# A decoder layer on one core: GpSimd out of the two branch projections, operands split in whole quarters

## The chip, the cores and the metric

The kernel runs on 1 core of one Trainium2 chip. The metric is the device time in microseconds of one execution. A core has TensorE (PE, matrix products), VectorE (DVE), ScalarE (ACT), GpSimd (POOL) and SyncE (SP, which issues transfers), each with its own queue of instructions that it takes in order; they wait for each other through semaphores.

## The reference, cut to what matters

One layer of a decoder, 512 tokens by 1024 channels, all in float32:

```
h = x @ w_in                                 # nine groups of 1024 columns
ya = gelu(ua) * spatial(va) * silu(za)       # branch A
yb = rms_norm(diff_attention(q, k, v)) * silu(zb)   # branch B
merged = sigmoid(ga) * (ya @ w_branch_a) + sigmoid(gb) * (yb @ w_branch_b)
ple = sigmoid(x @ w_ple_gate) * (p @ w_ple)
out = layer_norm(alpha * x + merged @ w_out + ple)
```

## The kernel before, in words

**Products in three parts.** Each float32 operand is split into a high part (rounded to fp32r by ScalarE with a Copy activation) and a low part (what is left, a VectorE subtraction). A product of two operands is then three matrix products: high by high, high by low, low by high (`three`). The weights stream from HBM in units of 128 x 1024 (512 KB) into eight buffers `wr`, and are split into `wh` and `wl` (lines 409 and 412, `spread`), four buffers each. Where the text says product, it means one such TensorE instruction of 512 columns.

**Seven steps for eight.** Most projections of 512 x 1024 by 1024 x 1024 are done by `quad`: each operand is cut into quarters (11, 12, 21, 22), and seven block products of quarters and sums of quarters replace eight. A stage has seven steps of 24 products, 168 in all. The left operand needs four of its quarters' sums besides three quarters. For x, ya and yb they are

```
S1 = q21 - q22,  S2 = S1 - q11,  N4 = S2 + q12,  S3 = q11 - q21
```

and each is split into high and low as well. `xh` and `xl` hold x in quarters; once a quarter of x (and later of yb) is read for the last time, it is overwritten with a quarter of yb (and later of ya). The four sums stand in the tiles `xs` (`ys` is the same pair), slots 0 to 3. The sums of the weights' quarters are made in HBM ahead of time, or in the `wr` buffer itself by a transfer that adds the next quarter to it; GpSimd issues these accumulating transfers (`follow`, line 384) as soon as the low part of the old weights is made.

**The order of the work.** The tail of the kernel is a chain of stages: ga, gb (gates from x, whose sigmoids go to HBM), pg (the embedding's gate from x), ple (48 products with p), wb (yb by w_branch_b), wa (ya by w_branch_a), out (192 products of 512 columns and 48 of 256). All other work hangs on a clock that counts products: `later(n, f)` runs `f`, which appends its instructions to the engines' queues, after n more products have been issued. So a position, such as 84 in pg, says where an instruction stands in its engine's queue in relation to the products; an engine may still run ahead of or behind TensorE.

**The steps around the change.** `cut_part` splits half a quarter (128 x 512): ScalarE writes the high part, and four products later VectorE the low part (line 1211). `add` makes half a sum on GpSimd (line 1223), in place of a quarter of `ua` (which holds ya) or `yb`. In a stage, `block` (line 665) combines two results on VectorE and calls `done` two products later: a sigmoid on ScalarE for ga, gb and pg (lines 1197 and 1265); in wb a product with the gate (`mb_done`, line 1316, GpSimd for two blocks of eight); in wa `merge` (lines 1349 and 1350), a product with the gate and an addition of the wb result, with the additions for the first two token groups and two of the products on GpSimd. `MERGE` products after that, `merge_turn` transposes the block on TensorE (line 1356) into bank po or tr, from which ScalarE (line 1359) and VectorE (line 1360) write the parts of out's left operand. The gates come back from HBM through `load_gates` (line 1323, 512 KB for two token groups), ln_g and ln_b through `load_last` (line 1341), and x is added to `base` by four accumulating transfers of GpSimd (line 1293).

The positions of all this stand in constants, one or two numbers for each quarter:

```
YA22, YA_S1, YA_S3, YA_CUT_S1 = (170, 177), (180, 188), (196, 204), (200, 207)
YA11, YA12, YA_S2, YA_N4 = (26, 33), (50, 57), (44, 52), (68, 76)
```

The first line counts from pg's start (168 and more is in ple), the second from wb's start.

Of the kernel before, what the change touches and what calls it, by code (L numbers as in the profile page):

```python
# [25 lines left out]
NT = T // P  # L26
# [219 lines left out]
def hybrid_layer(ctx: ExitStack, tc: tile.TileContext, a, out: bass.AP):  # L246
    nc = tc.nc
    pe, dve, act, pool, sp = nc.tensor, nc.vector, nc.scalar, nc.gpsimd, nc.sync
# [238 lines left out]
    xh = big.tile([P, KT, T], F32R, name="xh", tag="X0")  # L487
    xl = big.tile([P, KT, T], F32R, name="xl", tag="X1")
# [137 lines left out]
    def pairs(turn):  # L626
        one, two = [pp(), pp()], [pp(), pbank("tx", 1)]
        return (one, two)[not turn], (one, two)[turn], [pbank("sc", 2) for _ in range(2)]

    def of_parts(h, l, k0, t0):  # L630
        def at(t, k):
            ts = slice(t0, t0 + 2 * P) if t is None else slice(t0 + t * P, t0 + (t + 1) * P)
            return h[:, k0 + k, ts], l[:, k0 + k, ts]

        return at

    def of_sum(parts, c):
        def at(t, k):
            ts = slice(0, 2 * P) if t is None else slice(t * P, (t + 1) * P)
            return parts[0][:, c, k, ts], parts[1][:, c, k, ts]  # L640

        return at

    def operands(h, l, parts, last=4):

        s1, s2, n4, s3 = parts if callable(parts[0]) else [of_sum(parts, c) for c in range(4)]
        return (of_parts(h, l, 0, 0), of_parts(h, l, 4, 0), s1, n4, s2, s3, of_parts(h, l, last, 2 * P))

    def quad(name, left, banks, place, done):
# [12 lines left out]
        def block(c, t, first, second, op, spare):  # L662
            z = place(c, t)
            z = spare if z is None else z
            dve.tensor_tensor(out=z, in0=first, in1=second, op=op)  # L665
            later(2, done, c, t, z, z)

        goes_on = name in GOES_ON

# [34 lines left out]
        for i, (bank, first, after) in enumerate(steps):  # L704
            w = next_pair(name, i)
            for t in range(2):
                if name == "zq":
                    for j, k in ((j, k) for j in range(2 - t) for k in range(4)):
                        h, l = w[k // 2]
# [3 lines left out]
                else:  # L713
                    for k in range(4):
                        h, l = w[k // 2]
# [246 lines left out]
    for k in range(KT):  # L962
        if k % 2 == 0:
            h, l = next_unit("kq")
# [14 lines left out]
    ua = big.tile([P, KT, T], F32, name="ua", tag="U")  # L979
# [10 lines left out]
    yb = []  # L990
# [28 lines left out]
    late = ctx.enter_context(tc.tile_pool(name="late", bufs=1, side="right"))  # L1019
# [182 lines left out]
    quad("ga", of_x, pairs(False), lambda c, t: None, gate_done("ga"))  # L1202
    ys = xs

    def part_of(tiles, k, t, part):
        return (tile[:, 4 * k + 2 * part:4 * k + 2 * part + 2, t * 2 * P:(t + 1) * 2 * P] for tile in tiles)

    def cut_part(source, where, part):
        h, l = part_of((xh, xl), *where, part) if where in ((0, 0), (1, 0), (0, 1), (1, 1)) else where(part)
        act.activation(h, source, AF.Copy)  # L1210
        later(CUT_LOW, lambda: dve.tensor_tensor(out=l, in0=source, in1=h.bitcast(F32), op=OP.subtract))

    def cut_yb(k, t, where, part):
        source, = part_of((yb[0],), k, t, part)
        cut_part(source, where, part)

    def cut_ya(k, t, where, part):
        source, = part_of((ua,), k, t, part)
        cut_part(source, where, part)

    def add(tile, to, op, x, y, part):
        (z,), (x,), (y,) = (part_of((tile,), *q, part) for q in (to, x, y))
        pool.tensor_tensor(out=z, in0=x, in1=y, op=op)

    def add_ya(*what):
        add(ua, *what)

    def add_yb(*what):
        add(yb[0], *what)

    def slot(c):
        return lambda part: (tile[:, c, 2 * part:2 * part + 2, :] for tile in ys)

    alone = []

    def first_sum(part):
        if not alone:
            alone.extend(late.tile([P, 4, 2 * P], F32R, name="ya" + n, tag=n) for n in "gb")
        return (tile[:, 2 * part:2 * part + 2, :] for tile in alone)

    def of_first_sum(t, k):
        return tuple(tile[:, k, t * P:(t + 1) * P] for tile in alone)

    def in_parts(fn, ats, *what):
        for part, n in enumerate(ats):
            later(n, fn, *what, part)

    in_parts(cut_yb, YB22, 1, 1, (0, 1))
    in_parts(add_yb, YB_S1, (1, 1), OP.subtract, (0, 1), (1, 1))
    in_parts(add_yb, YB_S3, (0, 1), OP.subtract, (0, 0), (0, 1))  # L1250
# [12 lines left out]

    def embedding_gate(c, t, z, source):
        act.activation(z, source, AF.Sigmoid)

    in_parts(cut_yb, YB11, 0, 0, (0, 0))
    in_parts(cut_yb, YB12, 1, 0, (1, 0))
    in_parts(add_yb, YB_S2, (0, 0), OP.subtract, (1, 1), (0, 0))
    in_parts(add_yb, YB_N4, (1, 0), OP.add, (0, 0), (1, 0))  # L1270
    in_parts(cut_yb, YB_CUT_S1, 1, 1, slot(0))
    in_parts(cut_yb, YB_CUT_N4, 1, 0, slot(2))
    in_parts(cut_yb, YB_CUT_S2, 0, 0, slot(1))
    in_parts(cut_yb, YB_CUT_S3, 0, 1, slot(3))
    in_parts(cut_ya, YA22, 1, 1, (1, 1))
    in_parts(add_ya, YA_S1, (1, 1), OP.subtract, (0, 1), (1, 1))
    in_parts(add_ya, YA_S3, (0, 1), OP.subtract, (0, 0), (0, 1))
    in_parts(cut_ya, YA_CUT_S1, 1, 1, first_sum)
    quad("pg", of_x, pairs(False), lambda c, t: base[:, t, c * T:(c + 1) * T], embedding_gate)


    gate = {}
# [14 lines left out]
    for c in (1, 0):  # L1297
        h, l = next_unit("ple")
# [8 lines left out]
    mb = []  # L1307
# [20 lines left out]
    in_parts(cut_ya, YA11, 0, 0, (0, 0))  # L1328
    in_parts(cut_ya, YA12, 1, 0, (1, 0))
    in_parts(add_ya, YA_S2, (0, 0), OP.subtract, (1, 1), (0, 0))  # L1330
    in_parts(add_ya, YA_N4, (1, 0), OP.add, (0, 0), (1, 0))
    in_parts(cut_ya, YA_CUT_S3, 0, 1, slot(0))
    in_parts(cut_ya, YA_CUT_N4, 1, 0, slot(2))
    in_parts(cut_ya, YA_CUT_S2, 0, 0, slot(1))
    quad("wb", operands(xh, xl, ys, 0), pairs(True), place_b, mb_done)

    norm_last = []
# [4 lines left out]

    later(LAST_NORM[0], load_last, "ln_g", "g")
    later(LAST_NORM[1], load_last, "ln_b", "b")

    def merge(c, t, z, source):
        early = t < NT // 2
        by = pool if early and c else dve
        by.tensor_tensor(out=z, in0=source, in1=gate.pop(("ga", c, t)), op=OP.mult)
        (pool if early else dve).tensor_tensor(out=z, in0=z, in1=mb[0][:, t, c * T:(c + 1) * T], op=OP.add)  # L1350
        later(MERGE["early" if early else c], merge_turn, c, t, z)

    def merge_turn(c, t, m):
        bank = pbank("tr" if t % 2 else "po", 1)
# [5 lines left out]
        later(3, lambda: dve.tensor_tensor(out=xl[:, at[0], at[1]], in0=turned,  # L1360
                                           in1=xh[:, at[0], at[1]].bitcast(F32), op=OP.subtract))
# [27 lines left out]
    for those in ((0, 1), (2, 3)):  # L1389
        banks = {t: pbank("sc", 2) for t in those} if those[0] else {0: pp(), 1: pbank("tx", 1)}  # L1390
        for k in range(KT):
# [9 lines left out]
            h, l = units[k // 2]  # L1401
# [10 lines left out]
    for t in range(NT):  # L1412
        ts = slice(t * P, (t + 1) * P)
        n = T if t < NT - 1 else T // 2
        for j in range(T // n):
            bank = pp()
            for k in range(KT):
# [4 lines left out]
                h, l = units[k // 2]  # L1422
# [46 lines left out]
```

## Time and profile before

| | |
|---|---|
| median of 3 runs | 621.21 us (620.9 to 624.6) |
| the profiled execution | 622.56 us, of which 620.8 us is the span of the trace |
| granted TensorE clock, mean | 0.996 |
| busy in the span | PE 607.7, DVE 470.4, ACT 338.3, POOL 156.6 us |
| stages by TensorE's starts | pg from 432.09, wb from 482.80, wa from 522.38 us; out's second group from 580.36 us |

Times in rows of the profile are microseconds from the start of the span. A row of the timeline has the start, the duration, the engine, the line, the operation and out<-in; in brackets stands how long the engine idled before it and what ended that. A row of the table by stretches has, for each engine, its busy time and its number of instructions, then the granted clock, the DMA engines' busy share and GB/s. Matrix products overlap each other, so a busy TensorE may still lose time, which is seen in the distance of two starts.

### The profile page before, as it was taken

The numbers are of one execution on the slowest core, as the hardware profiler recorded it, in microseconds if no ns is written. First come the engines' busy times: TensorE is split into PE (matmuls) and PEld (weight loads), VectorE is DVE, ScalarE is ACT, GpSimd is POOL, SyncE is SP. The second block draws the span as 40 slices with busy tenths as digits, with TensorE's granted clock in tenths as the row PEclk, the third lists the DMA queues.
The fourth block names the chain that finished last, engine by engine and source line by source line (L and its number), as shares of the span: only waits on it lengthen the run. The fifth ranks groups of instructions, "written<-read, shape, count | busy, mean of one in ns | idle before, by whom it ended". The sixth has DMA issues, their size and how long they took to land.

```text
span 620.8 us, 8616 instructions
## 1 busy us (share of the span) xinstructions
PE 607.7 (98%) x3012; PEld 508.5 (82%) x3012; DVE 470.4 (76%) x778; ACT 338.3 (54%) x542; POOL 156.6 (25%) x156
## 2 busy tenths in 40 slices
PE   9999999999999999999999999999999999998995
PEld 6888888888888888888899988888887787776884
DVE  6995687878888765748578987678799788658476
ACT  6656664645645654478665665546676554543200
POOL 1234011332432630230102121141423152443011
PEclk9999999999999999999999999999999999999998
DMA  8789889679797597668898898967976487999102
GB/s 288 237 242 190 259 288 268 246 188 290 267 255 273 177 295 223 160 183 300 272 311 191 244 226 241 234 173 232 232 205 195 178 235 208 255 224 267 33 34 102
DMA packets 45631, 138.52 MB, mean 223 GB/s; under 512 B 6036, under 2 KB 7188, under 8 KB 45268
## 3 DMA queue, kind: packets, MB, share of 16 engines
q1 hardware_dynamic: 35092, 102.71, 46.4%
q0 software_dynamic: 9920, 34.87, 30.7%
q8 instruction: 24, 0.39, 0.3%
q10 hardware_dynamic: 576, 0.39, 0.2%
q14 instruction: 19, 0.16, 0.1%
HBM read 118.95 MB, written 30.54 MB: 241 GB/s over the span
## 4 chain that ended last, share of the span: by engine, by line
PE 85%; DMA 6%; DVE 4%; issue 3%; ACT 1%; POOL 1%; DVEq 0%; SPq 0%; POOLq 0%; ACTq 0%
PE ps_pp L280 52%; PE ps_sc L280 15%; PE ps_tx L280 6%; PE ps_sc L801 3%; DMA wr<-in_w 3%; PE ps_po L846 3%; DMA gates<-gate_ga 1%; DVE wl L412 1%; PE ps_tr L835 1%; PE ps_po L280 1%; PE ps_tr L280 1%; DMA wr<-ws_wb 1%; DVE base L1290 1%; PE ps_tr L1172 1%; PE ps_po L1172 1%
## 5 line engine op out<-in xcount | busy, mean ns | idle before, releaser
L412 DVE TENSOR_TENSOR wl<-wr,wh 128x1024 fp32r<-128x1024 f32 (+1 forms) x143 | 190.2, 1334 | 45.6 <-ACT wh L409 43.4
L409 ACT ACTIVATE wh<-wr 128x1024 fp32r<-128x1024 f32 (+1 forms) x143 | 147.1, 1033 | 72.9 <-PE ps_sc L280 29.0
L280 PE MATMUL ps_pp<-xh,wh 128*128 128x512 f32 (+1 forms) x276 | 109.3, 397 | 0.0
L280 PE MATMUL ps_pp<-xl,wh 128*128 128x512 f32 (+1 forms) x276 | 107.0, 388 | 0.1
L280 PE MATMUL ps_pp<-xh,wl 128*128 128x512 f32 (+1 forms) x276 | 105.5, 383 | 0.0
L280 PE MATMUL ps_pp<-wh,xh 128*128 128x512 f32 (+1 forms) x168 | 64.0, 381 | 0.3 <-DVE s L665 0.2
L280 PE MATMUL ps_pp<-wh,xl 128*128 128x512 f32 (+1 forms) x168 | 64.2, 382 | 0.0
L280 PE MATMUL ps_pp<-wl,xh 128*128 128x512 f32 (+1 forms) x168 | 64.0, 381 | 0.0
L814 ACT ACTIVATE p<-p,sth 128x128 f32<-128x128 f32 (+3 forms) x64 | 35.5, 556 | 46.6 <-DVE sth L812 46.5
L384 POOL DMA_DIRECT2D wr<-in_w x34 | 29.6, 872 | 122.1 <-DVE wl L412 118.1
L280 PEld LDWEIGHTS ps_pp<-xh,wl 128*128 128x128 f32 x276 | 52.1, 189 | 8.9 <-DVE wl L307 0.2
L280 PEld LDWEIGHTS ps_pp<-xh,wh 128*128 128x128 f32 x276 | 52.0, 189 | 8.5 <-ACT wh L306 0.5
L280 PEld LDWEIGHTS ps_pp<-xl,wh 128*128 128x128 f32 x276 | 52.1, 189 | 8.3 <-DVE xl L307 0.4
L746 POOL TENSOR_TENSOR hl<-m,hl 128x512 fp32r<-128x512 f32 x16 | 25.1, 1627 | 54.4 <-ACT hl L741 54.4
L280 PEld LDWEIGHTS ps_pp<-wh,xh 128*128 128x128 f32 x168 | 31.6, 188 | 7.3 <-DVE s L665 0.6
L280 PEld LDWEIGHTS ps_pp<-wl,xh 128*128 128x128 f32 x168 | 31.6, 188 | 6.2 <-DVE wl L412 0.4
L280 PEld LDWEIGHTS ps_pp<-wh,xl 128*128 128x128 f32 x168 | 31.6, 188 | 5.7
L808 DVE CUSTOM_DVE_ANT_0 p<-ps_sc,mask 128x128 f32<-128x128 f32 (+3 forms) x64 | 30.9, 483 | 6.3 <-PE ps_sc L801 6.3
L280 PE MATMUL ps_sc<-wl,xsh 128*128 128x512 f32 x88 | 34.5, 392 | 0.6 <-DVE wl L412 0.6
L280 PE MATMUL ps_sc<-wh,xsh 128*128 128x512 f32 x88 | 34.3, 390 | 0.0
L280 PE MATMUL ps_sc<-wh,xsl 128*128 128x512 f32 x88 | 34.2, 389 | 0.0
L280 PE MATMUL ps_pp<-wh,xsh 128*128 128x512 f32 x80 | 31.4, 393 | 0.1
(315 smaller groups left out, 1268.1 us busy)
## 6 DMA issues: line engine op xcount, KB each, us to landing
wr<-in_w SPq DMA_DIRECT2D x81, 512.0 KB, 4.7
wr<-in_w POOLq DMA_DIRECT2D x30, 512.0 KB, 6.2
k<-hl SPq DMA_DIRECT2D x16, 256.0 KB, 5.4
q<-hl SPq DMA_DIRECT2D x16, 256.0 KB, 4.1
ws_va<-in_w POOLq DMA_DIRECT2D x8, 512.0 KB, 10.3
wr<-ws_va SPq DMA_DIRECT2D x8, 512.0 KB, 4.3
wa<-in_w POOLq DMA_DIRECT2D x6, 512.0 KB, 7.2
kx<-hl SPq DMA_DIRECT2D x12, 256.0 KB, 5.4
```

What stands on the lines that cost most here:

```text
L280: pe.matmul(ps, s, m, start=start, stop=stop, skip_group_check=read_within)
L384: pool.dma_start(out=raw[u][:, :n], in_=weights(STEPS[FOLLOWS[u]][1], n), accum_op=OP.add)
L409: act.activation(h, raw[u][:, :width(STEPS[u][0])], AF.Copy)
L412: dve.tensor_tensor(out=l, in0=raw[u][:, :width(STEPS[u][0])], in1=h.bitcast(F32), op=OP.subtract)
L746: pool.tensor_tensor(out=hl[:, 3 - j, :], in0=m[2 * j], in1=hl[:, j, :].bitcast(F32), op=OP.subtract)
L801: pe.matmul(sc[m][:, :n], q[:, m, i * P:(i + 1) * P], kk[:, m, :n], start=o == 0, stop=o == 1)
L808: dve.tensor_tensor_reduce(out=pr[m][:, :n], in0=sc[m][:, :n], in1=mask[:, T - n:], scale=-(DK ** -0.5), scalar=3e38, op0=OP.add, op1=OP.m ...
L814: act.activation(pr[m][:, :n], pr[m][:, :n], AF.Exp, bias=st[:, m:m + 1], scale=-1.0, accum_out=st[:, 2 + m:3 + m])
L835: pe.transpose(tr[:, j * P:(j + 1) * P], ad[:, j * P:(j + 1) * P], ident)
L846: pe.matmul(po[:, i * P:(i + 1) * P], at[:, j * P:(j + 1) * P], v[:, j, h * P:(h + 1) * P], start=j == 0, stop=j == i)
L1172: pe.matmul(sa[:, t * P:(t + 1) * P], va[:, t, g * P:(g + 1) * P], aux[0][:, 0, g, :], start=True, stop=True)
L1290: dve.scalar_tensor_tensor(out=z, in0=bank, scalar=1.0 / ALPHA, in1=z, op0=OP.mult, op1=OP.mult)
```

## The change

The two branch projections wb and wa no longer use GpSimd for arithmetic: the products with the gates and the additions in `mb_done` and `merge` are all VectorE's, and ya's sums S2 and N4, made in wb, are whole VectorE operations (an int in place of a pair of positions, `combine`). The sums of yb, and S1 and S3 of ya, stay on GpSimd in halves; the two of ya move from ple into pg. A quarter is split in one piece (128 x 1024) instead of two halves, for ya and yb alike.

Places and positions change too. The split ya22 goes to the tiles `yag` and `yab` in pg, and S1 takes its natural place in `xh` and `xl` in wb; before, S1 was in those tiles and ya22 in its natural place. So wa's third step reads S1 from `xh`/`xl` and its last reads ya22 from `yag`/`yab`. The split of yb's S3 moves from pg (150) to wb's product 10; those of ya's N4 and S2 move from wb into wa's products 4 and 28. The sigmoids of ga, gb and pg are queued 8 products after their block instead of 2. p is loaded at pg's product 34 for 64 and split at 60 and 72 for 104 and 116. ln_g and ln_b are loaded at out's products 4 and 16 for wa's 100 and 130. `MERGE` has a number for each block.

```
+SIGMOIDS = ('ga', 'gb', 'pg')
-YB22, YB_S1, YB_S3 = (60, 72), (80, 92), (104, 116)
-YB11, YB12, YB_S2, YB_N4 = (26, 33), (50, 57), (46, 58), (70, 82)
-YB_CUT_S1, YB_CUT_N4, YB_CUT_S2, YB_CUT_S3 = (75, 82), (101, 108), (124, 131), (150, 157)
-YA22, YA_S1, YA_S3, YA_CUT_S1 = (170, 177), (180, 188), (196, 204), (200, 207)
-YA11, YA12, YA_S2, YA_N4 = (26, 33), (50, 57), (44, 52), (68, 76)
-YA_CUT_S3, YA_CUT_N4, YA_CUT_S2 = (78, 85), (98, 105), (122, 129)
+YB22, YB_S1, YB_S3 = 60, (80, 92), (104, 116)
+YB11, YB12, YB_S2, YB_N4, YB_SUMS = 25, 49, (34, 46), (58, 70), (75, 101, 124, 226)
+YA22, YA_S1, YA_S3 = 36, (84, 96), (108, 120)
+YA11, YA12, YA_S2, YA_N4, YA_SUMS = 26, 50, 54, 64, (19, 76, 172, 196)
-LAST_NORM = (100, 130)
-MERGE = {'early': 24, 1: 23, 0: 22}
+LAST_NORM = (172, 184)
+MERGE = (36, 36, 25, 27), (40, 40, 68, 62)
...
-            later(2, done, c, t, z, z)
+            later(8 if name in SIGMOIDS else 2, done, c, t, z, z)
...
+    def quarter(tile, k, t):
+        return tile[:, 4 * k:4 * k + 4, t * 2 * P:(t + 1) * 2 * P]
+
+    def natural(k, t):
+        return lambda: (quarter(xh, k, t), quarter(xl, k, t))
...
+    def apart():
+        alone.extend(late.tile([P, 4, 2 * P], F32R, name="ya" + n, tag=n) for n in "gb")
+        return alone
...
+    def split_quarter(n, source, where):
+        def high():
+            h, l = where()
+            act.activation(h, source, AF.Copy)
+            later(CUT_LOW, lambda: dve.tensor_tensor(out=l, in0=source, in1=h.bitcast(F32), op=OP.subtract))
+
+        later(n, high)
+
+    def combine(ats, to, op, x, y):
+        def part(engine, e):
+            z, a0, a1 = (q[:, e] for q in (to, x, y))
+            engine.tensor_tensor(out=z, in0=a0, in1=a1, op=op)
+
+        if isinstance(ats, int):
+            later(ats, part, dve, slice(0, 4))
+        else:
+            for i, n in enumerate(ats):
+                later(n, part, pool, slice(2 * i, 2 * i + 2))
...
-            later(40 + 12 * k, cut, phl[0][:, 0, k, :], phl[0][:, 1, k, :], pt)
+            later(26 + 12 * k, cut, phl[0][:, 0, k, :], phl[0][:, 1, k, :], pt)
-    later(64, load_p)
+    later(34, load_p)
...
+    split_quarter(YB11, yb11, natural(0, 0))
+    combine(YB_S2, yb11, OP.subtract, yb22, yb11)
+    split_quarter(YB12, yb12, natural(1, 0))
+    combine(YB_N4, yb12, OP.add, yb11, yb12)
+    for n, source, c in zip(YB_SUMS, (yb22, yb12, yb11, yb21), (0, 2, 1, 3)):
+        split_quarter(n, source, slot(c))
+    split_quarter(YA22, ya22, apart)
+    combine(YA_S1, ya22, OP.subtract, ya21, ya22)
+    combine(YA_S3, ya21, OP.subtract, ya11, ya21)
     quad("pg", of_x, pairs(False), lambda c, t: base[:, t, c * T:(c + 1) * T], embedding_gate)
...
-        by = pool if c == 1 and t < 2 else dve
-        by.tensor_tensor(out=z, in0=source, in1=gate.pop(("gb", c, t)), op=OP.mult)
+        dve.tensor_tensor(out=z, in0=source, in1=gate.pop(("gb", c, t)), op=OP.mult)
...
+    split_quarter(YA_SUMS[0], ya22, natural(1, 1))
+    split_quarter(YA11, ya11, natural(0, 0))
+    combine(YA_S2, ya11, OP.subtract, ya22, ya11)
+    split_quarter(YA12, ya12, natural(1, 0))
+    combine(YA_N4, ya12, OP.add, ya11, ya12)
+    for n, source, c in zip(YA_SUMS[1:], (ya21, ya12, ya11), (0, 2, 1)):
+        split_quarter(n, source, slot(c))
     quad("wb", operands(xh, xl, ys, 0), pairs(True), place_b, mb_done)
...
-        early = t < NT // 2
-        by = pool if early and c else dve
-        by.tensor_tensor(out=z, in0=source, in1=gate.pop(("ga", c, t)), op=OP.mult)
-        (pool if early else dve).tensor_tensor(out=z, in0=z, in1=mb[0][:, t, c * T:(c + 1) * T], op=OP.add)
-        later(MERGE["early" if early else c], merge_turn, c, t, z)
+        dve.tensor_tensor(out=z, in0=source, in1=gate.pop(("ga", c, t)), op=OP.mult)
+        dve.tensor_tensor(out=z, in0=z, in1=mb[0][:, t, c * T:(c + 1) * T], op=OP.add)
+        later(MERGE[c][t], merge_turn, c, t, z)
...
-    of_ya = [of_first_sum, of_sum(ys, 1), of_sum(ys, 2), of_sum(ys, 0)]
-    quad("wa", operands(xh, xl, of_ya), pairs(False), lambda c, t: None, merge)
+    of_ya = (of_parts(xh, xl, 0, 0), of_parts(xh, xl, 4, 0), of_parts(xh, xl, 4, 2 * P),
+             of_sum(ys, 2), of_sum(ys, 1), of_sum(ys, 0), of_apart)
+    quad("wa", of_ya, pairs(False), lambda c, t: None, merge)
```

More of the change, by code (lines that the diff above doesn't have):

```diff
@@ L1203, in hybrid_layer @@
     ys = xs
[L1205 to L1229, printed above, removed]
+    def quarter(tile, k, t):
+        return tile[:, 4 * k:4 * k + 4, t * 2 * P:(t + 1) * 2 * P]
+    def natural(k, t):
+        return lambda: (quarter(xh, k, t), quarter(xl, k, t))
@@ L1231, in slot @@
     def slot(c):
-        return lambda part: (tile[:, c, 2 * part:2 * part + 2, :] for tile in ys)
+        return lambda: (ys[0][:, c], ys[1][:, c])
     alone = []
[L1236 to L1241, printed above, removed]
-        return tuple(tile[:, k, t * P:(t + 1) * P] for tile in alone)
-    def in_parts(fn, ats, *what):
-        for part, n in enumerate(ats):
-            later(n, fn, *what, part)
@@ L1248, in hybrid_layer, with of_apart @@
-    in_parts(cut_yb, YB22, 1, 1, (0, 1))
-    in_parts(add_yb, YB_S1, (1, 1), OP.subtract, (0, 1), (1, 1))
-    in_parts(add_yb, YB_S3, (0, 1), OP.subtract, (0, 0), (0, 1))
+    def apart():
+        alone.extend(late.tile([P, 4, 2 * P], F32R, name="ya" + n, tag=n) for n in "gb")
+        return alone
+    def of_apart(t, k):
+        return tuple(tile[:, k, t * P:(t + 1) * P] for tile in alone)
+    def split_quarter(n, source, where):
[4 more added lines that the diff above has]
+        later(n, high)
@@ new lines, in combine @@
+    def combine(ats, to, op, x, y):
[7 more added lines that the diff above has]
+                later(n, part, pool, slice(2 * i, 2 * i + 2))
+    yb11, yb12, yb21, yb22 = (quarter(yb[0], k, t) for t in range(2) for k in range(2))
+    ya11, ya12, ya21, ya22 = (quarter(ua, k, t) for t in range(2) for k in range(2))
@@ L1251, in hybrid_layer @@
+    split_quarter(YB22, yb22, natural(0, 1))
+    combine(YB_S1, yb22, OP.subtract, yb21, yb22)
+    combine(YB_S3, yb21, OP.subtract, yb11, yb21)
     quad("gb", of_x, pairs(True), lambda c, t: None, gate_done("gb"))
@@ L1265, in embedding_gate @@
         act.activation(z, source, AF.Sigmoid)
[L1267 to L1278, printed above, removed]
+    split_quarter(YB11, yb11, natural(0, 0))
[7 more added lines that the diff above has]
+    combine(YA_S3, ya21, OP.subtract, ya11, ya21)
     quad("pg", of_x, pairs(False), lambda c, t: base[:, t, c * T:(c + 1) * T], embedding_gate)
@@ L1327, in hybrid_layer @@
         later(n, load_gates, *what, i % 2)
[L1328 to L1334, printed above, removed]
+    split_quarter(YA_SUMS[0], ya22, natural(1, 1))
[5 more added lines that the diff above has]
+        split_quarter(n, source, slot(c))
     quad("wb", operands(xh, xl, ys, 0), pairs(True), place_b, mb_done)
```

## The prediction

> **What bounds the kernel now.** I read the head of the page first, then the chain that ended last, then TensorE's timeline by its starts.
>
> ```profile
> span 620.8 us, 8616 instructions
> ...
> PE 607.7 (98%) x3012; PEld 508.5 (82%) x3012; DVE 470.4 (76%) x778; ACT 338.3 (54%) x542; POOL 156.6 (25%) x156
> ```
>
> ```profile
> 444.04 10.88 PE ps_sc L280 x48
> ```
>
> TensorE is busy for 98% of the span, but one product's 0.39 us overlaps the next, so busy time hides gaps. The chain's piece gives the pace: 48 products in 10.88 us, 0.2267 us each. A stage of 168 products cannot take less than 38.08 us. The first products of wb, of wa and of out's second group stand here, and one transpose with the product behind it:
>
> ```profile
> 482.80 0.39 PE L280 MATMUL ps_pp<-wh,xh 128*128 128x512 f32 x1
> ...
> 522.38 0.39 PE L280 MATMUL ps_pp<-wh,xh 128*128 128x512 f32 x1
> ...
> 540.57 0.60 PE L1356 MATMUL ps_tr<-ident,s 128*128 128x128 f32 x4
> 540.92 0.48 PE L280 MATMUL ps_sc<-wl,xsh 128*128 128x512 f32 x1
> ...
> 580.36 0.39 PE L280 MATMUL ps_sc<-wh,xh 128*128 128x512 f32 x1
> ```
>
> wb takes 39.58 us, 1.5 over its floor. From 522.38 to 580.36 lie 168 + 48 products (48.97 us) and eight groups of transposes at 0.35 us (2.8 us): 57.98 us, 6.2 over. So 7.7 us is all that these stages can give. Four gaps (start to start, less 0.23) make most of it:
>
> ```profile
> 495.05 0.39 PE L280 MATMUL ps_sc<-wh,xsh 128*128 128x512 f32 x1
> 496.04 0.50 PE L280 MATMUL ps_sc<-wl,xsh 128*128 128x512 f32 x1 [0.60 <-DVE wl L412]
> ...
> 536.09 0.39 PE L280 MATMUL ps_sc<-wh,yag 128*128 128x512 f32 x1
> 537.29 0.66 PE L1356 MATMUL ps_po<-ident,s 128*128 128x128 f32 x4 [0.81 <-POOL s L1350]
> ...
> 559.12 0.39 PE L280 MATMUL ps_pp<-wl,xh 128*128 128x512 f32 x1
> 560.53 0.66 PE L1356 MATMUL ps_tr<-ident,s 128*128 128x128 f32 x4 [1.03 <-POOL s L1350]
> ...
> 569.04 0.39 PE L280 MATMUL ps_tx<-wl,xh 128*128 128x512 f32 x1
> 570.94 0.66 PE L1356 MATMUL ps_po<-ident,z 128*128 128x128 f32 x4 [1.51 <-DVE xl L1360]
> ```
>
> That is 0.76, 0.97, 1.18 and 1.67 us, 4.6 in all: a weight part late from VectorE, two transposes that wait for GpSimd's additions, and a transpose whose bank VectorE had not yet read.
>
> **GpSimd's price to VectorE.** Next I put POOL and DVE side by side:
>
> ```profile
> 412.26 4.25 POOL L1223 TENSOR_TENSOR yb<-yb 128x512 f32<-128x512 f32 x3
> 412.81 4.79 DVE L412 TENSOR_TENSOR wl<-wr,wh 128x1024 fp32r<-128x1024 f32 x1 [2.26 <-ACT wh L409]
> ```
>
> ```profile
> 479.76 1.29 POOL L1223 TENSOR_TENSOR ua<-ua 128x512 f32<-128x512 f32 x1
> ...
> 479.76 0.68 DVE L1290 SCALAR_TENSOR_TENSOR base<-ps_sc,base 128x512 f32<-128x512 f32 x1
> ```
>
> The weight part that takes 1.21 us elsewhere took 4.79: it ended 1.1 us after three GpSimd operations in a row. Line 1290, with one operand in PSUM, kept its 0.68 beside such an operation. So a GpSimd half quarter (1.29 us alone) holds up a VectorE operation with two SBUF operands by up to 1.3 us, more than the half would cost on VectorE.
>
> **The change, part by part.** Position n is n products into a stage.
>
> *wb and wa without GpSimd.* Two products with gates, four additions and two more products with gates move to VectorE at 0.69 us each, 5.5 us; four half sums become two whole ones, 2.4 us (1.21 each, the weight part's size). Twelve GpSimd operations go, each of which could hold VectorE for up to 1.3 us. VectorE's load is therefore about equal, and transposes now wait for an addition of 0.69 us, 36 to 68 products after its merge. The gaps 0.97 and 1.18 go; I take 0. The gap 0.76 comes from a VectorE that left ple full:
>
> ```profile
> core 0: us, PE busy (x) PEld busy (x) DVE busy (x) ACT busy (x) POOL busy (x), PEclk, DMA share, GB/s
> 433.30:443.30 10.00, 10.00 (x50) 8.43 (x49) 6.47 (x8) 5.91 (x9) 1.27 (x2) 1.00 1.01 262
> 443.30:453.30 10.00, 10.00 (x46) 8.29 (x45) 9.49 (x7) 7.31 (x11) 6.18 (x6) 1.00 0.83 205
> 453.30:462.30 9.00, 9.00 (x42) 7.44 (x41) 8.29 (x9) 6.14 (x9) 2.10 (x2) 1.00 0.94 227
> ...
> 471.60:482.70 11.10, 11.10 (x49) 8.99 (x49) 10.94 (x14) 5.37 (x8) 6.08 (x4) 1.00 0.51 169
> ```
>
> In ple VectorE was busy for 10.94 of 11.10 us; four half splits and four GpSimd halves leave it. But wb's first 64 products then carry six weight parts, four splits, two sums and two gate products: 12 x 1.14 + 2 x 0.6 = 14.9 us, and start near 2 us, for a part that is needed at product 79 (17.9 us). It just fits; 0 to 0.8, I take 0.3.
>
> *The last gap.* There VectorE stood at line 1349 for gates asked late, and the reading of the bank stood behind it:
>
> ```profile
> 544.79 0.86 POOL L384 DMA_DIRECT2D wr<-in_w  x1 [1.20 <-DVE wl L412]
> ...
> 560.42 3.55 POOL L1293 DMA_DIRECT2D base<-in_x  x4
> ```
>
> ```profile
> 559.80 0.39 SPq L1323 DMA_DIRECT2D gates<-gate_ga  x1
> ```
>
> ```profile
> 568.87 0.69 DVE L1349 TENSOR_TENSOR z<-ps_pp,gates 128x512 f32<-128x512 f32 x1 [1.60 <-DMA gates<-gate_ga]
> ```
>
> The load issued at 559.80 landed near 568.8, 9 us, beside four transfers of x issued at 560.42. GpSimd's queue will have nothing between 544.79 and these four, so they start some 15 us earlier, behind the last accumulation in their own queue, and SP's loads of ln_g and ln_b (LAST_NORM) go past the gates into out. The gates come sooner; the turns move from out's products 11 and 23 to 14 and 28, those of the other half column behind them to 35 and 41, so no bank is wanted again within 13 products. 0 to 1.7, I take 0.5. The remaining 7.7 - 4.6 = 3.1 us lie in small pieces, part of them bank waits that VectorE causes; I take 0.7 of them back.
>
> Gain: 4.6 - 0.3 - 0.5 + 0.7 = 4.5 us.
>
> *pg.* Into pg come ya22's split (36), all of S1 and S3 of ya on GpSimd (84 to 120), and the two cuts of p (60 and 72 for 104 and 116); out of it goes yb's S3. These lines are pg's VectorE before, and the start of its fifth step (the product's own line):
>
> ```profile
> 443.81 3.62 DVE L412 TENSOR_TENSOR wl<-wr,wh 128x1024 fp32r<-128x1024 f32 x1 [0.61 <-ACT wh L409]
> ...
> 447.35 0.68 DVE L1211 TENSOR_TENSOR xl<-yb,xh 128x512 fp32r<-128x512 f32 x1
> 447.95 1.21 DVE L412 TENSOR_TENSOR wl<-wr,wh 128x1024 fp32r<-128x1024 f32 x1
> 449.09 1.78 DVE L1211 TENSOR_TENSOR xl<-yb,xh 128x512 fp32r<-128x512 f32 x1
> ...
> 452.53 3.09 DVE L412 TENSOR_TENSOR wl<-wr,wh 128x1024 fp32r<-128x1024 f32 x1
> ...
> 458.49 1.21 DVE L412 TENSOR_TENSOR wl<-wr,wh 128x1024 fp32r<-128x1024 f32 x1
> ```
>
> ```profile
> 454.75 0.39 PE L280 MATMUL ps_pp<-wh,xsh 128*128 128x512 f32 x1
> ```
>
> Starts lie 0.60 us (half) and 1.14 us (whole) apart. The part at 458.49, ready at 459.7, is position 108's: the sixth step's second unit, needed 31 products after 454.75, at 461.8. Lead: 2.1 us. Ahead of it the new queue holds five whole splits for seven halves (5.7 for 4.2 us, 1.5 more), one more cut of p (0.6), and 7.5 GpSimd halves at 1.3 us (9.8; the first of S2 falls half beside a PSUM operation) where the old one lost 2.4, 1.1 and 1.9 us to four of them (the excess of 443.81, 449.09 and 452.53): 4.4 more. That is 6.5, less some 0.6 of idle time, 5.9. In program order S1's first half comes ahead of the accumulation at 84, and the other three follow it in a row, as the three at 412.26 did, just when positions 100 and 108 are due. TensorE then waits 5.9 - 2.1 = 3.8 us in pg. If the added halves fall into idle time, 1.5 us is left, inside the lead, and the cost is 0. Ends 0 and 3.8; I take 3.8, for the row at 412.26 has the same instructions in the same order. What VectorE owes is paid off by ple, which is relieved.
>
> *Costed at nothing.* Sigmoids at 8 for 2: ScalarE waited 10.3 us for VectorE in ga and gb, hidden under products; if that cover went, the price would be those waits. The loads of p go earlier in SP's queue, past nothing that TensorE needs soon. ln_g, asked at out's fourth product, waits there for wa's last step, whose operand lies in the tile that it overwrites; behind it stand ln_b and a weight load for out's second half, and if that were wanted at once, the price would be ln_g's wait.
>
> ```profile
> ACT s L1197 <- DVE s L665: 10.3, 9, 3.4
> ```
>
> Whole splits save starts (1.14 for 2 x 0.60), counted above. S1 of ya in its natural place and ya22 apart change no product; its last read merely lets the turns of the second column go earlier than the last step.
>
> **Sum.** -4.5 + 3.8 = -0.7 us. Against the profiled execution 622.56 - 0.7 = 621.9; that execution lies 1.35 over the median of the runs, so I forecast 621.21 - 0.7 = 620.5. I treat 1% (6.2 us) as what a measurement of this kernel can tell from no change.
>
> **Rivals.** *pg does not starve* (0.28): VectorE had 3.5 us idle from 433.3 to 443.3, and gb's stretched part stopped no product. Then 621.2 - 4.5 = 616.7; with all 7.7 us regained 613.5.
>
> *Slower: the early transfers of x* (0.11). Four times 512 KB at the 227 GB/s of the row from 453.30 are 9.2 us of traffic put into wa's sixth and seventh steps, beside out's weights and the last gates. If the queues share alike, half of it, 4.6 us, is added to the gates' 9: 13.6. Asked at 140 and held some 3 products by a weight part, they have 39 products and a group of transposes (9.2 us) less two VectorE operations (1.4) until the turn at 182. Beyond 7.8 us they decide; 5.8 us go to TensorE in place of the 0.5: 625.8. Against it: before, the four came 0.6 us after that load and shared with it already, and 1 MB of ln_g and ln_b leaves the stage.
>
> *Accumulations kept waiting* (0.03). More VectorE work on two SBUF operands in wa could hold up GpSimd's descriptors: one weight part's 1.14 us on each of three accumulated steps, with nothing to spare, makes 3.4 us, 623.9.
>
> ```profile
> L384 POOL DMA_DIRECT2D wr<-in_w x34: 837/861/1065, 50.2 to 544.8; - x34
> ```
>
> All 34 issues took 837 to 1065 ns, with VectorE busy or not. [...]
>
> **From these.** Forecast 0.58, the rivals 0.28, 0.11 and 0.03. The range is 615.8 to 624.6: below, pg's cost at 0 and 0.9 us more of the small pieces; above, wb's 0.8, the gates' 1.7 and none of the small pieces (622.9), and part of the way to the slower rivals. Faster by over 1% (under 615.0) needs nearly all 7.7 us and no cost in pg: 0.05. Slower by over 1% (over 627.4) needs pg's full cost, no gain and the early transfers: 0.03. Within: 0.92.
>
> **What would show it.** Right: weight parts of 4 us or more around pg's positions 84 to 110, TensorE gaps before "wl" there of 3 to 4 us, pg longer by 2 us or more, no wait for POOL at the transposes, wa within 1 us of its floor with transposes. Wrong: pg as long as before; a DVE wait for gate_ga over 2 us; a gap in wb's fourth step over 0.8 us. A lock that lets VectorE in between two GpSimd operations would make the pg term, and so the forecast, too slow.

## The result: 628.1 us, slower by 1%, and the profile after

The changed kernel takes 628.1 us in the median of four runs (627.35 to 629.4); the kernel before, on the same chip, 621.06 (620.75 to 624.6). The ratio is 1.0095, interval 1.0067 to 1.0124. I had forecast 620.5 and a range up to 624.6: wrong, and on the other side. The profiled execution took 627.35 us against 622.56, so 4.8 us have to be found in the trace. The head of the page after:

```profile
span 625.5 us, 8563 instructions
...
PE 608.3 (97%) x3012; PEld 511.2 (82%) x3012; DVE 470.0 (75%) x774; ACT 337.5 (54%) x528; POOL 136.7 (22%) x144
```

TensorE's busy time is as before, GpSimd's is down by 20 us, VectorE's is equal: the change did to the loads what it says. The time lies in TensorE's gaps. Its timeline after, at the two places that were lengthened, with the first product of out's second group at the end (columns: start and length in us, engine, line, operation, output and inputs; in brackets the idle time and what ended it):

```profile
462.15 0.39 PE L279 MATMUL ps_pp<-wh,xsh 128*128 128x512 f32 x1
464.00 0.50 PE L279 MATMUL ps_pp<-wl,xsh 128*128 128x512 f32 x1 [1.47 <-DVE wl L411]
...
465.04 0.39 PE L279 MATMUL ps_pp<-wh,xsl 128*128 128x512 f32 x1
466.70 0.50 PE L279 MATMUL ps_pp<-wh,xsh 128*128 128x512 f32 x1 [1.27 <-ACT s L659]
...
568.13 0.39 PE L279 MATMUL ps_pp<-wl,xh 128*128 128x512 f32 x1
573.07 1.09 PE L1345 MATMUL ps_po<-ident,z 128*128 128x128 f32 x4 [4.56 <-DVE z L1339]
...
574.38 0.63 PE L279 MATMUL ps_tx<-wh,xh 128*128 128x512 f32 x1
574.81 0.63 PE L279 MATMUL ps_tx<-wl,xh 128*128 128x512 f32 x1
...
585.03 0.39 PE L279 MATMUL ps_sc<-wh,xh 128*128 128x512 f32 x1
```

Start to start, less 0.23, the gaps are 1.62 and 1.43 us in pg and 4.71 us in out; behind the last one two products start 0.43 us apart where 0.23 is the pace. By stages, from the starts of their first products (for out, up to its second group):

| stage | before | after | difference | predicted |
|---|---|---|---|---|
| pg | 39.56 | 44.05 | +4.5 | +3.8 |
| ple | 11.15 | 11.15 | 0 | 0 |
| wb | 39.58 | 38.13 | -1.45 | -0.5 |
| wa | 43.93 | 40.03 | -3.90 | -2.8 with the 0.7 of small pieces |
| out, first group | 14.05 | 19.85 | +5.80 | -1.2 |

Ahead of pg the kernel after is 0.27 us sooner, and from the second group on both need 40.45 us. The other rows went the way that was forecast, pg near its size, wb and wa further than predicted. The one that turned the sign is the last row. VectorE's timeline after shows what stands at its head, and the queues of GpSimd and SP what came ahead of the load:

```profile
454.20 3.68 DVE L411 TENSOR_TENSOR wl<-wr,wh 128x1024 fp32r<-128x1024 f32 x2
457.80 5.01 DVE L1226 TENSOR_TENSOR xsl<-yb,xsh 128x1024 fp32r<-128x1024 f32 x1
462.74 1.21 DVE L411 TENSOR_TENSOR wl<-wr,wh 128x1024 fp32r<-128x1024 f32 x1
...
571.51 0.69 DVE L1338 TENSOR_TENSOR z<-ps_pp,gates 128x512 f32<-128x512 f32 x1 [6.12 <-DMA gates<-gate_ga]
```

```profile
454.06 1.60 POOL L1233 TENSOR_TENSOR ua<-ua 128x512 f32<-128x512 f32 x1
457.04 0.89 POOL L383 DMA_DIRECT2D wr<-in_w  x1 [1.39 <-DVE wl L411]
457.66 4.06 POOL L1233 TENSOR_TENSOR ua<-ua 128x512 f32<-128x512 f32 x3
...
546.48 3.94 POOL L1285 DMA_DIRECT2D base<-in_x  x4
```

```profile
559.58 0.43 SPq L1314 DMA_DIRECT2D gates<-gate_ga  x1
```

The four transfers of x go out at 546.48 instead of 560.42, right behind GpSimd's last accumulation. The gates of ga are asked at 559.58, as before (559.80), but VectorE can use them only at 571.51, after 11.9 us instead of 9. It stood 6.12 us for them; the transpose at 573.07 stood behind it. The transfers of x were still on their way when the gates were asked (their number, the shortest, median and longest issue in ns, the first and last start; then the shortest, median and longest time from issue to landing in us):

```profile
L1285 POOL DMA_DIRECT2D base<-in_x x4: 1229/1760/2292, 546.5 to 548.1; - x4
...
DMA to landing us min/median/max: 12.5/17.4/22.1
```

None of the four had landed before 559.0, and the slowest took until about 570. In pg the three halves of 457.66 to 461.72 and the split of 5.01 us that covers them are the stretch that the prediction drew, and the weight part at 462.74 is the late one.

The table of stretches after shows the rest of out's 5.8 us (columns: the stretch, its length, busy time and instructions of PE, PEld, DVE, ACT and POOL, granted clock, DMA share, GB/s):

```profile
565.20:568.20 3.00, 3.00 (x15) 2.42 (x13) 0.19 (x1) 1.98 (x3) 0.00 (x0) 1.00 1.04 274
568.20:573.00 4.80, 0.31 (x2) 0.00 (x0) 1.46 (x3) 0.00 (x0) 0.00 (x0) 0.81 1.03 406
573.00:578.00 5.00, 4.93 (x14) 4.10 (x15) 4.69 (x6) 0.60 (x1) 0.00 (x0) 0.50 0.19 75
578.00:585.00 7.00, 7.00 (x37) 5.80 (x37) 2.15 (x4) 1.80 (x3) 0.00 (x0) 1.00 0.00 0
```

In the gap the DMA engines are full, moving 406 GB/s. Behind it the granted clock is 0.50 for five microseconds: 14 instructions where 37 fit into the seven after them. A gap of 4.7 us costs a second time, here some 2.4 us.

### The profile page after: what moved, and what is told of

The parts are those of the page before. It is cut to its first block, busy times and chain, and to the rows that moved or that the text cites. A ratio compares the mean times of both kernels' runs of the same rounds, so it can differ in the third digit from the quotient of the medians.

```text
span 625.5 us, 8563 instructions
## 1 busy us (share of the span) xinstructions
PE 608.3 (97%) x3012; PEld 511.2 (82%) x3012; DVE 470.0 (75%) x774; ACT 337.5 (54%) x528; POOL 136.7 (22%) x144
## 4 chain that ended last, share of the span: by engine, by line
PE 80%; issue 9%; DMA 5%; DVE 4%; ACT 1%; POOL 0%; DVEq 0%; SPq 0%; POOLq 0%; ACTq 0%
PE ps_pp L279 49%; PE ps_sc L279 13%; PE ps_tx L279 7%; PE ps_sc L800 3%; PE ps_po L845 3%; DMA wr<-in_w 2%; DMA gates<-gate_ga 2%; DVE wl L411 2%; PE ps_tr L834 1%; DVE xsl L1226 1%; PE ps_po L279 1%; PE ps_tr L279 1%; PE ps_tr L1171 1%; PE ps_po L1171 1%; DMA wr<-ws_wb 1%
## 5 line engine op out<-in xcount | busy, mean ns | idle before, releaser
L411 DVE TENSOR_TENSOR wl<-wr,wh 128x1024 fp32r<-128x1024 f32 (+1 forms) x143 | 181.0, 1274 | 39.6 <-ACT wh L408 37.2
L279 PE MATMUL ps_pp<-wh,xh 128*128 128x512 f32 (+1 forms) x160 | 61.0, 381 | 0.6 <-DVE base L664 0.6
L279 PE MATMUL ps_pp<-wh,xl 128*128 128x512 f32 (+1 forms) x160 | 61.4, 384 | 0.0
L279 PE MATMUL ps_pp<-wl,xh 128*128 128x512 f32 (+1 forms) x160 | 60.9, 381 | 0.0
L279 PEld LDWEIGHTS ps_pp<-wl,xh 128*128 128x128 f32 x160 | 30.3, 189 | 5.6
L279 PE MATMUL ps_pp<-wl,xsh 128*128 128x512 f32 x80 | 31.4, 393 | 2.0 <-DVE wl L411 2.0
```

Of the source, the lines that this page charges most:

```text
L279: pe.matmul(ps, s, m, start=start, stop=stop, skip_group_check=read_within)
L411: dve.tensor_tensor(out=l, in0=raw[u][:, :width(STEPS[u][0])], in1=h.bitcast(F32), op=OP.subtract)
```

## The experiments

Two theories had to be tested. **The transfers of x:** issued early, they share the DMA engines with the gates' load, and so make out's gap. **The sums in pg:** ya's halves on GpSimd (S1, S3) starve VectorE, and so make pg's gaps. Rivals: out's gap comes from VectorE's load in wa, which the change took over from GpSimd, or from the four weight loads that stand ahead of the gates in SP's queue; or pg is longer for the whole splits, whoever adds the halves. All runs are set against the kernel before on the same chip, which took 621.85 to 622.64 us in the median of those of several rounds. "Out" is out's first group, as in the table above.

**x in wb.** The four transfers of x are asked in wb instead of out.

```diff
-RESIDUE = (2, 8, 26, 32)
+RESIDUE = (4, 24, 100, 120)
+    for t, n in enumerate(RESIDUE):
+        later(n, residue, t)
     quad("wb", ...)
...
     quad("wa", ...)
-    for t, n in enumerate(RESIDUE):
-        later(n, residue, t)
```

> The changed kernel, with the four transfers that add x to base queued in wb (positions 4, 24, 100, 120) instead of out. Theory A (the transfers of x, issued early in wa because GpSimd has nothing else left, share the DMA engines with the last gates): the gates land within 8 us of their issue, VectorE's wait for them falls from 6.1 us to under 1, the gap ahead of the transposes in out from 4.7 to under 1.5 us, the granted clock stays at 1.0 there, and the time falls by 5 to 6.5 us to about 622. Rival B (the gates are late because of the four weight loads ahead of them in SP's queue): gap 4 us or more, time within 1 us of 628.

Measured: 622.57 us, ratio 1.0001 (0.9977 to 1.0025). Out takes 12.76 us, without a gap and at full clock: 7.1 us less than after. The four weight loads and VectorE's work in wa are as after, so neither made the gap. The same transfers now stand before another load. At wb's last block, which VectorE reaches when wa has begun, its timeline of this run has:

```profile
528.60 0.69 DVE L1307 TENSOR_TENSOR mb<-ps_pp,gates 128x512 f32<-128x512 f32 x1 [4.49 <-DMA gates<-gate_gb]
```

These are the last gates of gb, asked at 520.93, 9.5 us after two transfers of x. They landed after 7.6 us, in the profile after in 4.9; TensorE lost 0.74 us in wa to that. So x's transfers made out's gap, and moving them moves the delay to whichever load comes next.

**Sums on VectorE.** ya's S1 and S3 whole on VectorE, at the same places.

```diff
-YA22, YA_S1, YA_S3 = 36, (84, 96), (108, 120)
+YA22, YA_S1, YA_S3 = 36, 84, 108
```

> The changed kernel, with ya's S1 and S3 in pg as two whole VectorE operations instead of four GpSimd halves. Theory C (the shared access to SBUF: each GpSimd half stops VectorE for 1.3 us): VectorE has 2 x 1.14 us in place of 4 x 1.3, so pg's gaps fall from 4.5 us to 1 to 2, and the time by about 3 us. Rival D (it is the amount of VectorE work moved into pg: the split of ya22 and the earlier cuts of p): two more VectorE operations make it worse, gaps 4.5 to 6.5 us.

Measured: 624.88 us, ratio 1.0038 (1.0009 to 1.0067); pg 41.28 instead of 44.05, out still 19.82 with a gap of 4.91. VectorE's timeline there:

```profile
458.85 1.21 DVE L1233 TENSOR_TENSOR ua<-ua 128x1024 f32<-128x1024 f32 x1
459.98 1.22 DVE L411 TENSOR_TENSOR wl<-wr,wh 128x1024 fp32r<-128x1024 f32 x1
```

A whole sum costs 1.2 us there, and the part behind it keeps its 1.22. On GpSimd the three halves alone stretched one split from 1.2 to 5.0. Three gaps of 0.5 to 0.7 us stay: what is left, 1.7 us, goes with ya22's split and the two sums that VectorE has here. Both causes hold, GpSimd's the larger with 2.8 of 4.5 us.

**Sums asked for in ple.** The same halves on GpSimd, at positions in ple; ya22's split left in pg.

```diff
-YA22, YA_S1, YA_S3 = 36, (84, 96), (108, 120)
+YA22, YA_S1, YA_S3 = 36, (180, 188), (196, 204)
```

> The changed kernel, with ya's S1 and S3 back in ple on GpSimd, in halves (180 to 204). Theory C: pg keeps 0.7 us more VectorE work than before against a lead of 2.1, so pg's gaps fall from 4.5 us to under 0.5; ple and wb lose at most 1 us; time about 624. Rival D: gaps in pg stay above 3 us.

Measured: 630.65 us in a single execution, pg 45.68. The expectation failed. GpSimd's timeline of this run, and then TensorE's:

```profile
455.64 0.88 POOL L383 DMA_DIRECT2D wr<-in_w  x1 [1.39 <-DVE wl L411]
456.21 5.36 POOL L1233 TENSOR_TENSOR ua<-ua 128x512 f32<-128x512 f32 x4
```

```profile
461.25 0.39 PE L279 MATMUL ps_pp<-wh,xsh 128*128 128x512 f32 x1
463.86 0.50 PE L279 MATMUL ps_pp<-wl,xsh 128*128 128x512 f32 x1 [2.22 <-DVE wl L411]
```

All four halves ran in a row in the middle of pg. A position orders the queue; it is no time. GpSimd had nothing else behind its accumulation at 455.64 and their sources were ready, so it did them at once, now four in a row instead of three. The gap at the late weight part is 2.4 us, not 1.6. Unwanted, this is a larger dose of the suspected cause, and that gap grew with it. The other gaps shrank, though: pg's are 3.8 us in all against 4.5, and that pg is longer than after comes from the half clock behind them (shown at the end).

**Merges by GpSimd.** The products with gates and the additions in wb and wa go back to GpSimd, as before; MERGE stays as changed.

```diff
+        by = pool if c == 1 and t < 2 else dve          # mb_done
...
+        early = t < NT // 2                             # merge
+        by = pool if early and c else dve
...
+        (pool if early else dve).tensor_tensor(out=z, in0=z, ...)
```

> The changed kernel, with the products and additions of mb_done and merge back on GpSimd as before, all positions as changed. Theory A: GpSimd is held until its last addition near 560, so the transfers of x start 12 us or more later; the gates' wait falls to about 2 us and the gap in out from 4.7 to 1 to 2.5 us, while gaps of 1 to 3 us come back in wa; time 624 to 627. Rival B: the gap in out stays at 4 us or more, and the time rises above 629.

Measured: 622.07 us in a single execution, less than the 624 to 627 expected; pg 44.00, wa 42.02, out 12.80. GpSimd's and SP's timelines of this run:

```profile
559.69 2.14 POOL L1342 TENSOR_TENSOR s<-s,mb 128x512 f32<-128x512 f32 x1
561.78 3.54 POOL L1285 DMA_DIRECT2D base<-in_x  x4
```

```profile
561.15 0.38 SPq L1315 DMA_DIRECT2D gates<-gate_ga  x1
```

So this is what had held x's transfers back: the last addition of GpSimd's merge stood ahead of them in its queue, and the gates were asked 0.6 us before them. VectorE used these gates at 567.95, 6.8 us after they were asked, and did not wait for them. out's gap goes although x's code is untouched. In return wa pays 2.0 us, most of it one product that stood 1.3 us for VectorE's line 664.

**ya22 in ple.** With ya22's split at 170, the halves have no source before it.

```diff
-YA22, YA_S1, YA_S3 = 36, (84, 96), (108, 120)
+YA22, YA_S1, YA_S3 = 170, (180, 188), (196, 204)
```

> The changed kernel, with the split of ya22 at 170 (in ple) besides S1 and S3 on GpSimd at 180 to 204. Theory C, amended (a position does not hold GpSimd, which starts a half as soon as its queue and its sources allow; the halves stop VectorE wherever they run): S1 now depends on a split made in ple, so the four halves run there, beside VectorE's operations with a PSUM operand; pg's gaps fall from 4.5 us to under 0.7, out's gap stays at 4 to 5, time about 624. Rival D (the earlier cuts of p and the whole splits crowd pg): pg's gaps stay above 2 us.

Measured: 621.66 us in a single execution; pg 39.25 without a gap, ple 11.16, wb 38.08; out keeps a gap of 4.55 (18.96). GpSimd's timeline:

```profile
474.23 6.04 POOL L1233 TENSOR_TENSOR ua<-ua 128x512 f32<-128x512 f32 x4 [17.24 <-DVE yab L1226]
```

The halves now wait 17 us for their source and run in ple, where they cost TensorE nothing (11.16 us for 11.15): most of VectorE's operations there have an operand in PSUM, and the one weight part that fell among the halves took 1.35 us. pg's 4.5 us are these sums and this split, whole; the earlier cuts of p and the whole splits of yb, still in pg, cost it nothing.

**Both moves.** x in wb and the sums on VectorE, together.

```diff
-YA22, YA_S1, YA_S3 = 36, (84, 96), (108, 120)
+YA22, YA_S1, YA_S3 = 36, 84, 108
-RESIDUE = (2, 8, 26, 32)
+RESIDUE = (4, 24, 100, 120)     # and the loop before quad("wb"), as above
```

> The changed kernel, with the transfers of x in wb (4, 24, 100, 120) and with S1 and S3 of ya as whole VectorE operations in pg. Theories A and C add up: pg 41.3 us, out's first group 12.8 us, time 622.6 - 2.8 = 619.8, 0.3% under the kernel before. If the two are not independent (a pg without gaps meets later transfers), 621 to 623.

Measured: 619.81 us, ratio 0.9934 (0.9905 to 0.9963). Only the time of this run is read, not its stages. Against the two single moves (622.57 and 624.88, from 628.1) the gains of 5.5 and 3.2 us add up to 8.7; 8.3 were seen. In ratios to the kernel before on the same chip, 0.94% and 0.57% make 1.5%, and 1.6% were seen. Within what these times can tell, the two causes are separate.

**Sums late, x at wb's start.** All of ya22, S1, S3 whole on VectorE in late pg and ple, and the four transfers at the head of wb.

```diff
-YA22, YA_S1, YA_S3 = 36, (84, 96), (108, 120)
+YA22, YA_S1, YA_S3 = 136, 170, 190
-RESIDUE = (2, 8, 26, 32)
+RESIDUE = (4, 8, 12, 16)        # and the loop before quad("wb")
```

> The changed kernel, with all four transfers of x at wb's start (4 to 16), the split of ya22 at pg's 136 and S1 and S3 as whole VectorE operations in ple (170, 190). Theory C: pg within 0.8 us of 39.56, as VectorE's crowded part (positions 40 to 110) is free of them; theory A: out's first group at 12.8 us, and no gap in wa from late gates; wb 38.1, wa 40.1: 615 to 616.5. Against: four transfers at once delay the ready-made weights of wb, which then shows 0.5 to 2 us of gaps: up to 618.

Measured: 620.94 us, ratio 0.9953 (0.9920 to 0.9985); pg 39.42 and out 12.80, but wb 42.87. VectorE's timeline:

```profile
497.02 0.69 DVE L1307 TENSOR_TENSOR mb<-ps_pp,gates 128x512 f32<-128x512 f32 x1 [4.12 <-DMA gates<-gate_gb]
497.63 1.21 DVE L411 TENSOR_TENSOR wl<-wr,wh 128x1024 fp32r<-128x1024 f32 x1
```

The expected 615 to 618 us were missed. It is the same delay a third time, at gb's first gates, which landed after 13.4 to 14.2 us where they took 4.1 to 5.6 in the profile after, and this time a weight part stood right behind the waiting product: TensorE stopped for 3.2 us, and products at half pace followed.

**The kernel before, with x in wb.** The edit of the first experiment, in the kernel before.

> The kernel before, with the transfers of x queued in wb (4, 24, 100, 120). Theory A: the last gates no longer share with them, VectorE does not wait for gate_ga, the gap of 1.67 us in out goes, time about 1.5 us less (619.6). Rival B: gap and time unchanged.

Measured: 621.41 us, ratio 0.9959 (0.9930 to 0.9987). The gap of 1.67 us of before is gone and out takes 12.34, but wa is 0.6 longer. The last gates landed after 6.0 us instead of 8.9. So the gates' lateness that the prediction had read in the kernel before came from x's transfers too.

**x behind the gates.** A one-column GpSimd operation that reads the last gates is queued ahead of x's transfers, so that they leave only when the gates have landed; all else as changed.

```diff
+    def hold():
+        pool.tensor_tensor(out=small([P, 1], "hold", 1), in0=mhalf[:, 0:1],
+                           in1=pairs_of_gates[:, 1, 0, 0:1], op=OP.mult)
+
+    later(GATES[-1] + 2, hold)
```

> The changed kernel, with one GpSimd operation of one column that reads the last gates, queued ahead of the four transfers of x, so that these start when the gates have landed. Theory A: the gates land within 7 us of their issue, VectorE waits for them under 1 us, out's first group takes 12.8 us in place of 19.85 at a clock of 1.0, and nothing is lost in wb or wa (38.1 and 40.0); pg keeps its 4.5 us; time about 621. Rival B: the gates still take 11 us or more, time 627 or more. Against the fix: the transfers of x land too late for out's first residual, which would show as a VectorE wait near the end.

Measured: 621.61 us, ratio 0.9993 (0.9976 to 1.0010); wa 40.08, out 12.79, pg 44.63. SP's and GpSimd's timelines:

```profile
562.22 0.39 SPq L1314 DMA_DIRECT2D gates<-gate_ga  x1
```

```profile
566.48 0.99 POOL L1321 TENSOR_TENSOR hold<-mhalf,gates 128x1 f32<-128x1 f32 x1 [17.53 <-DMA gates<-gate_ga]
567.42 3.60 POOL L1285 DMA_DIRECT2D base<-in_x  x4
```

Without x's transfers the load lands in 4.3 us, with them ahead of it in 11.9. With them right behind it the price is smaller: at most 6.8 us in the run with merges by GpSimd, and 8.9 in the kernel before, which has ln_b's load ahead of it too and takes 6.0 without x. That is the price of sharing the DMA engines, shown by one small instruction. wb's and wa's gains stay whole.

**Both cures.** ya22 and its halves in ple, and x behind the gates: the two diffs above, together.

> Both at once: the split of ya22 at 170 with S1 and S3 on GpSimd at 180 to 204, and the transfers of x behind the last gates. Stages by theories A and C: pg 39.3, ple 11.15, wb 38.1, wa 40.0, out's first group 12.8 us, that is 7 us less than the kernel before (0.989): about 614 to 615. If the two do not add up, 617 to 619.

Measured: 615.57 us, ratio 0.9902 (0.9874 to 0.9930), faster than either kernel. The page of this run, then its table of stretches, pg to out's first group:

```profile
span 613.3 us, 8564 instructions
...
PE 604.6 (99%) x3012; PEld 510.0 (83%) x3012; DVE 464.9 (76%) x774; ACT 337.7 (55%) x528; POOL 139.2 (23%) x145
```

```profile
431.60:470.60 39.00, 39.00 (x178) 32.45 (x177) 31.49 (x29) 28.05 (x35) 9.99 (x8) 1.00 0.82 220
470.60:481.80 11.20, 11.20 (x50) 9.01 (x48) 9.16 (x11) 4.50 (x5) 6.04 (x4) 1.00 0.43 149
481.80:519.90 38.10, 38.10 (x169) 31.56 (x168) 30.30 (x32) 21.65 (x25) 3.51 (x4) 1.00 0.71 224
519.90:560.00 40.10, 40.10 (x186) 33.14 (x185) 31.64 (x37) 20.61 (x26) 6.62 (x8) 1.00 0.91 235
560.00:572.80 12.80, 12.80 (x66) 10.60 (x65) 8.66 (x13) 4.38 (x7) 3.40 (x4) 1.00 0.98 227
```

TensorE's busy time is the length of every stretch, at full clock: no stage from pg on has a gap over 0.12 us left. The two cures singly gave 6.5 and 6.4 us (the second in a single execution), together 12.5.

## Why the prediction was wrong

**The step that failed is "the last gap".** It says of x's transfers that "they start some 15 us earlier", and concludes "The gates come sooner ... 0 to 1.7, I take 0.5". The first is right (14 us), the second wrong: 4.71 us of gap and 2.4 of half-speed products, 7.1 us over the 12.8 that this group needs, where I took 0.5. The conclusion counted what would no longer be issued beside the load and not what would still be on its way when the load was issued. The gates were in fact asked 0.2 us sooner only. The same paragraph had a row that hinted at it: 9 us for that load with x's transfers issued 0.6 us behind it. Without them it takes 6.0 in the kernel before and 4.3 in the changed one, as the runs showed; I took the transfers' leaving for a relief and gave no price to their being ahead.

**The slower rival was this case,** with its place and its mechanism. Its chance of 0.11 was too low, for the reason given against it: that before "the four came 0.6 us after that load and shared with it already". Sharing from behind and sharing from ahead are not the same: in the changed kernel at most 6.8 against 11.9 us. Its price, 5.8 us to TensorE, came from 13.6 us for the load by equal shares; the load took 11.9, which beyond its bound of 7.8 makes 4.1; the gap was 4.7. It lacked the fall of the clock: the half-speed products made 4.7 into 7.1. It also cancelled only the 0.5, and kept all other terms. And at 625.8 it lay outside the range, whose upper end of 624.6 left out a case that had been given more than a tenth.

**pg: right in its cause, and in its size partly by luck.** Predicted 3.8 us, measured 4.5; three halves in a row, a VectorE operation stretched to 5.0, the weight part of the sixth step late. The rival "pg does not starve" (0.28) is out. But the 3.8 were put down to the weight part alone. It made 1.62. Another 1.43 came from ScalarE's line 659, which stood behind a sigmoid that itself stood for VectorE; the list of waits after has that sigmoid:

```profile
ACT base L1260 <- DVE base L664: 6.9, 2, 5.7
```

The other 1.4 are two gaps of 0.72 at a part and at a bank. A late VectorE reached TensorE by three ways at once, and the sum matched only in total.

**wb and wa: right, and too low.** The gaps for GpSimd's additions went, as said (0 for 0.97 and 1.18), and wb's late part went altogether (I kept 0.3 of it). The small pieces gave more than the 0.7 of 3.1 that I took: 5.35 us in both stages against 3.3 predicted. In wb 38.13 us stand against a floor of 38.08. Here a VectorE that owed nothing left hardly a small gap either; I had no row for these and put them at a quarter.

**Accumulations kept waiting (0.03):** not seen. wa has no gap for them.

With that one term put right (out at its measured +5.8 instead of -1.2, 7.0 us) the forecast for the profiled execution would have been 621.9 + 7.0 = 628.9. Measured were 627.35; the 1.6 between are what wb and wa gave beyond the forecast (2.0) and 0.27 ahead of pg, less pg's further 0.7.

## What to carry to other kernels

Work taken off an engine also takes away what held up the instructions queued behind it: list them, above all transfers, and ask of each what it will now share the DMA engines with. A bulky transfer that nobody needs soon is best tied to the landing of the urgent load, for which one small instruction that reads that load is enough; moved to "some earlier place", it delays the load that is there. And a place in program order holds an engine only as long as the instruction's sources or its queue do; where work must not run early, let its source come late.

## What the runs showed of the hardware

**The clock falls for a gap, and not only for a long one.** In the gap of 4.7 us TensorE's granted clock fell some 3 us after the last product (mean 1.00 from 568.2 to 570.0, 0.91 to 571.5, 0.50 from there to 578), so that products ran at half pace for about 5 us; behind 3.2 us (sums late) it was again 0.50, from 499 to 502. The gap of 1.67 us in the kernel before left it at full speed. But with the halves asked for in ple, two gaps of 2.4 and 1.4 us within 6 us gave this stretch of that run:

```profile
466.50:472.20 5.70, 5.65 (x13) 4.46 (x14) 4.82 (x6) 4.06 (x6) 0.00 (x0) 0.50 0.30 95
```

In the run with x behind the gates, pg's same two gaps (1.62 and 1.43) were followed by a mean clock of 0.76 from 466 to 473; in the profile after the same gaps left it at 1.00 there. So near this size it can fall either way, which may be part of the spread of the changed kernel's runs: the two of 628.74 and 629.4 us have a mean clock of 0.989, the two of 627.35 and 627.45 one of 0.992. Where the clock was lost in them is not shown. The Trainium skill (TensorE: Matmul & The Clock Gate, "Part 1: The HAM clock gate (the "warmup" mystery)") says that the array falls to half rate after an idle window of about 3.4 us and needs about as long a busy time to come back; half rate as the only step and the 4.7 us gap agree with this case, and the two shorter gaps in succession show that less than one such idle stretch was enough here.

**GpSimd operations back to back can leave VectorE no turn between them, but need not.** In the profile after, three halves of 4.06 us made one split 5.01 us long; before, three of 4.25 made a weight part 4.79. But the same profile after has, 10 us earlier:

```profile
447.60 3.86 POOL L1233 TENSOR_TENSOR yb<-yb 128x512 f32<-128x512 f32 x2 [2.37 <-DVE xl L1226]
```

```profile
447.98 2.32 DVE L411 TENSOR_TENSOR wl<-wr,wh 128x1024 fp32r<-128x1024 f32 x1
```

This weight part ended at 450.30, before the second half's end at 451.46, and the two halves took 3.86 us where two alone take 2.58: VectorE had its turn between them. In the run with both cures GpSimd and VectorE have in ple:

```profile
473.65 6.04 POOL L1233 TENSOR_TENSOR ua<-ua 128x512 f32<-128x512 f32 x4 [17.36 <-DVE yab L1226]
```

```profile
474.68 1.35 DVE L411 TENSOR_TENSOR wl<-wr,wh 128x1024 fp32r<-128x1024 f32 x1
...
477.78 0.69 DVE L1282 SCALAR_TENSOR_TENSOR base<-ps_sc,base 128x512 f32<-128x512 f32 x1 [0.56 <-PE ps_sc L279]
```

Here too a weight part got through in the midst of four halves, and the operation with one operand in PSUM kept its 0.69 us. The Trainium skill (SBUF — State Buffer, "Who interferes with whom") tells of an exclusive lock on a port pair that both engines share; the traces agree, each operation waiting for one of the other engine as a whole. The case named at the end of the prediction, a lock that lets VectorE in between two of them, did not come about at 457.66, where the term of pg was worked out, but it did in these two places. What decides who comes next is open.
